# Absorbed queries of a latent-attention kernel, split into high and low parts straight from PSUM by ScalarE and VectorE

## The chip, the cores and the metric

The kernel runs on one core of a Trainium2 chip. The metric is the time of one execution on the device in microseconds (us), as the median of three runs. The engines are named as in the profile: PE is TensorE (PEld its weight loads), DVE is VectorE, ACT is ScalarE, POOL is GpSimd, SP is SyncE.

## The reference, cut to what matters

Two layers of a diffusion backbone are computed for 1024 latent tokens and 128 prompt tokens. The first layer is multi-head latent attention with 16 heads; the change lies in it. Its scores need, for each head, the product of queries and keys, and the keys are an expansion of a compressed latent of 128 numbers:

```
q = (rms_norm(q_a, q_norm_g) @ w_qb).reshape(..., 16, 128 + 64)       # q_nope, q_rope
k_nope, v = split((c_kv @ w_kvb).reshape(..., 16, 128 + 128))
s = (einsum('bqhd,bkhd->bhqk', q_nope, k_nope)
     + einsum('bqhr,bkr->bhqk', q_rope, k_rope)) * MLA_SCALE
p = softmax_f32(s)
o = einsum('bhqk,bkhd->bqhd', p, v)
```

The kernel doesn't expand the keys. It multiplies the query weight of a head with the key weight of that head and applies the product to the low-rank query (256 numbers for each token). The result, an *absorbed query* of 128 numbers for each token and head, is multiplied with the latent itself.

## The kernel before

**Precision.** A float32 operand is split into a high part, rounded to the type fp32r, and a low part, the rest; a product is then three fp32r matmuls (`mm3`: high-high, high-low, low-high). `split_to(hi, lo, src, eng_lo)` (L148) does the split: ACT copies `src` to `hi` with the cast, and then the engine `eng_lo`, POOL unless another is named, subtracts `hi` from `src` and writes `lo` (the helper `sub`, L83).

**The units.** Latent attention runs from about 345 us to 1135 us as a loop over 64 units, unit k = 4 * head + u with u the quarter of 256 latent tokens. Each unit takes about 12.3 us (790 us by 64). While unit k is exponentiated and multiplied with the values, the scores of unit k + 1 are made, their running maximum is taken (`run_max`, L760 to L764 on DVE), the maximum is transposed by PE (`max_cols`, L769), reduced by DVE (L774), turned into a row by PE (L788) and subtracted from the scores by further matmuls (L800). The exponentials are split: cast by ACT (L812), subtraction by DVE (`lo`, L817). POOL adds them up (`sums`, L825 to L830). PE multiplies the last key blocks with the values as whole float32 numbers (L838, called v68 in the orders) and the others in split form (L88 ps_M, called v03 and v45).

**The order is written out.** In this loop every engine runs its instructions in the order in which the program issues them. The order is a string for each k % 8 (`ORDERS`), whose marks are steps: `s` scores, `m` the maximum, `e` the exponential, `h` and `l` the high and low part of the exponentials, `+` the sums, `v` the values, `M` and `L` the way of the maximum and of the row sums (`M0`, `L0` transposes, `M1`, `L1` reductions, `L2`, `L3` the split of the inverse), `F` and `O` the end of the unit before. The parts of the strings of k % 8 = 5 and 6 that matter here:

```
5: ... s2 P m2 T h1 +2 +3 s3 l1 h2 m3 P +4 p s4 m4 l2 v68 ES p  L0 M0 L1 M1 L2 v03 p A L3 ES ...
6: ... s2 p m2 T e4 h1 +2 +3 s3 l1 h2 m3 p +4 s4 m4 l2 v68 ES P M0 P L0 L1 M1 L2 v03 L3 ES A ...
```

**The side work.** The queries of the next heads are made in the gaps of that order, as a queue of items of the type `Work`: `prod` (matmuls into a PSUM bank), `evac` (what takes the result out) and `rest` (what is done with it later). `P` or `p` issues the `prod` of the next item, unless one still waits to be evacuated; `ES` or `EV` issues its `evac` with ACT or DVE as the engine `eng`; `A` issues one step of `rest`. For a head there is one `w_item` (the weight product), three `q_item`s (384 tokens of absorbed queries each: 6 matmuls of 384 columns), and for an even head three `rope_item`s (the rotary queries of two heads); items of the prompt's attention come between.

**One bank.** All these products go to PSUM banks with the tag `W`, and in this stage there is one of them (`psum_plan(M=2, W=1)`; with three of `S`, two of `T` and two of `M` all eight banks are taken). The next `prod` on PE waits until everything that reads the bank's last contents is done.

**The absorbed query before.** `evac` copies the bank to the SBUF tile `qt` (L566 through `copy_by`, L521). `parts`, which an `A` issues later, splits `qt` into the tiles `qA` (two heads' buffers in turn): ACT casts (L149), POOL subtracts (L83). For head 0 alone DVE subtracts (`G_ = V if h == 0 else G`); head 0 is made ahead of the loop, in the region from about 322 to 340 us, where the order is not written out. Items of head 1 to 15, 45 in all, lie in the loop.

Of the kernel before, what the change touches and what calls it, by code (L numbers as in the profile page):

```python
# [11 lines left out]
F32 = mybir.dt.float32  # L12
# [7 lines left out]
P = 128  # L20
# [37 lines left out]
def hybrid_step(ctx: ExitStack, tc: tile.TileContext, i, o):  # L58
    nc = tc.nc
    V, S, G = nc.vector, nc.scalar, nc.gpsimd  # L60
# [15 lines left out]
    def bank(tag):  # L76
        return (psum if tag in "ST" else ps_now["pool"]).tile([P, 512], F32, tag=tag, name=f"ps_{tag}",
                                                               bufs=n_banks[tag])
# [3 lines left out]
    def sub(eng, out, a, b):  # L82
        eng.tensor_tensor(out, a, b, ALU.subtract)  # L83

    def mm3(ps, lhs, rhs, first=True, last=True):

        for n, (a, b) in enumerate(PASSES):
            nc.tensor.matmul(ps, lhs[a], rhs[b], start=first and n == 0, stop=last and n == 2)  # L88
# [59 lines left out]
    def split_to(hi, lo, src, eng_lo=G):  # L148
        S.copy(hi, src)  # L149
        sub(eng_lo, lo, src, hi.bitcast(F32))  # L150
# [369 lines left out]
    def copy_by(eng, out, src):  # L520
        (eng.copy if eng is S else eng.tensor_copy)(out, src)  # L521

    def head_work(h):

        w = {}
        G_ = V if h == 0 else G

        def pair_tiles(a, b, dt=F32):
            if h == 0:
                t = pg.tile([P, 1024], dt, tag="raw", name="w_raw", bufs=4)  # L530
                return t[:, 0:384], t[:, 384:768]
            return [p2.tile([P, 384], dt, tag=x, name=x, bufs=1) for x in (a, b) if x]
        wa = []
        hps[h] = hp = {}

        def w_item():
            c = {}

            def prod():
                wq, wk, w["r"] = head_w.pop(h)  # L540
                c["ps"] = bank("W")[:, :2 * LAT]
                for k in range(2):
                    mm3(c["ps"][:, k * P:(k + 1) * P], [wq[e][:, k * P:(k + 1) * P] for e in range(2)], wk)

            def evac(eng):
                c["t"] = p2a.tile([P, 384], F32, tag="qt", name="qt", bufs=2)[:, :2 * LAT]
                copy_by(eng, c["t"], c["ps"])
            def parts():
                wa.extend(p2a.tile([P, 2 * LAT], F32R, tag=f"wa{e}", name=f"wa{e}", bufs=1) for e in range(2))
                split_to(wa[0], wa[1], c["t"], G_)  # L550
                fresh.add(("wa", h))
            return Work(prod, evac, [parts])

        def q_item(g):
            c = {}
            sl = slice(g * 384, (g + 1) * 384)

            def prod():
                c["ps"] = bank("W")[:, :384]
                for k in range(2):  # L560
                    mm3(c["ps"], [wa[e][:, k * P:(k + 1) * P] for e in range(2)], [qaT[e][:, k, sl] for e in range(2)],
                        k == 0, k == 1)

            def evac(eng):
                c["t"] = p2a.tile([P, 384], F32, tag="qt", name="qt", bufs=2)
                copy_by(eng, c["t"], c["ps"])  # L566
            def parts():
                if g == 0:
                    hp["qA"] = qA_[h % 2]
                    if h % 2 == 1:  # L570
                        hp["q2"] = q2_[h % 3]
                split_to(hp["qA"][0][:, sl], hp["qA"][1][:, sl], c["t"], G_)
                there.add((h, g))
            return Work(prod, evac, [parts], ("wa", h))

        def rope_item(g):
            c = {}
            sl = slice(g * 384, (g + 1) * 384)
            n = 384 if g < 2 else 256
            ls = slice(g * 384, g * 384 + n)  # L580

            def prod():
                wr = w["r"]
                c["ps"] = bank("W")[:, :384]
                for k in range(2):
                    mm3(c["ps"], [wr[e][:, k * P:(k + 1) * P] for e in range(2)], [qaT[e][:, k, sl] for e in range(2)],
                        k == 0, k == 1)
                c["rC"], c["rS"] = pair_tiles("rC", "rS")
                dma(c["rC"][:, :n], i["ropeC"][:, ls])
                dma(c["rS"][:, :n], i["ropeS"][:, ls])  # L590

            def evac(eng):
                c["a"] = p2a.tile([P, 384], F32, tag="qt", name="qt", bufs=2)
                copy_by(eng, c["a"], c["ps"])

            def rotate():
                a, b = c["a"], pair_tiles("rp0", None)[0]
                V.stream_shuffle(b[:, :n], a[:, :n], [x ^ 16 for x in range(32)])
                G_.tensor_tensor(b[:, :n], b[:, :n], c["rS"][:, :n], ALU.mult)
                V.tensor_tensor(a[:, :n], a[:, :n], c["rC"][:, :n], ALU.mult)  # L600
                G_.tensor_tensor(a[:, :n], a[:, :n], b[:, :n], ALU.add)

            def parts():
                a = c["a"]
                t = pair_tiles("rp0", "rp1", F32R)
                split_to(t[0], t[1], a, V)
                if g == 0:

                    hp["q2"] = q2_[h % 3]
                q2 = q2_[h % 3], q2_[(h + 1) % 3]  # L610
                for e in range(2):
                    r = slice(e * 64, e * 64 + 64)
                    dma(q2[e][0][0:64, sl].bitcast(F32), t[0][r].bitcast(F32))
                    dma(q2[e][0][64:128, sl].bitcast(F32), t[0][r].bitcast(F32))
                    dma(q2[e][1][0:64, sl].bitcast(F32), t[1][r].bitcast(F32))
            return Work(prod, evac, [rotate, parts])
        return [w_item()] + [x(g) for g in range(3) for x in ([rope_item] if h % 2 == 0 else []) + [q_item]]
# [270 lines left out]
    p2a = es_a.enter_context(tc.tile_pool(name="p2a", bufs=1, side="right", reuse_waits="tile"))  # L888
# [122 lines left out]
    for k, (h, u) in enumerate(units):  # L1011
# [26 lines left out]
        for step in ORDERS[k % 8].split():  # L1038
# [5 lines left out]
            c, n = step[0], int(step[1:] or 0) if step[1:].isdigit() else step[1:]  # L1044
# [111 lines left out]
    for t in range(NT):  # L1156
        ps = bank("S")[:, :256] if t else early["ps"]
# [234 lines left out]
    for hf in range(2):  # L1392
        for t in range(NT):
            ps = bank("S")
# [391 lines left out]
    for k in range(-2, N):  # L1786
# [22 lines left out]
        for step in NORDER.split():  # L1809
            c, n = step[0], step[1:]  # L1810
# [159 lines left out]
```

## Time and profile before

| | |
|---|---|
| median of 3 runs | 2126.91 us (2126.76 to 2130.87) |
| the profiled execution | 2128.24 us |
| its span in the profile | 2126.5 us |
| PE busy | 2021.3 us, 95% of the span |
| DVE busy | 1358.8 us, 64% |
| ACT busy | 1045.9 us, 49% |
| POOL busy | 824.4 us, 39% |

The span runs from the first to the last instruction that the profile shows; 1.74 us of the profiled execution lie around it. A busy share is a mean over stages with different limits, and the change lies in one stage.

### The profile page before, as it was taken

Reading aid. Unit: us, or ns where it says so; the run is one execution under the profiler, and the core shown is the slowest. Engines: PE = TensorE matmul, PEld = TensorE weight load, DVE = VectorE, ACT = ScalarE, POOL = GpSimd, SP = SyncE. Lnnn points to the kernel's source line nnn. Section 1 sums busy time; section 2 is a strip of 40 time slices with the busy share of each in tenths; the row PEclk is TensorE's granted clock in tenths of the full one; section 3 lists DMA queues with packets and bytes.
Section 4 is the critical chain, followed back from the end, with each engine's and each line's share of the span. In section 5 each row is a group of like instructions: output and inputs, shape, how many; then the busy total and the mean of one; then the engine's idle time right before and its main releaser. Section 6 shows DMA issues by size and latency. Waiting matters only on the chain. (4 is left out here: it accounts for less than half of the span.)

```text
span 2126.5 us, 36852 instructions
## 1 busy us (share of the span) xinstructions
PE 2021.3 (95%) x12894; PEld 1856.7 (87%) x12894; DVE 1358.8 (64%) x2904; ACT 1045.9 (49%) x2430; POOL 824.4 (39%) x822
## 2 busy tenths in 40 slices
PE   8899998999999999999998899999999999999897
PEld 3799998888999998899997788899889999998686
DVE  5723885767787868686776645532116788888743
ACT  6555115554555555555554433433115666666621
POOL 1411224676676768776764300100002333333300
PEclk9999998999999999999999999999999999999899
DMA  8222763212121213121214624326324555556753
GB/s 300 91 74 94 239 174 85 60 50 69 50 76 45 80 32 96 55 80 32 76 31 149 220 103 136 103 100 202 122 104 147 181 178 178 175 176 199 212 156 90
DMA packets 177229, 256.43 MB, mean 121 GB/s; under 512 B 20946, under 2 KB 142578, under 8 KB 177044
## 3 DMA queue, kind: packets, MB, share of 16 engines
q1 hardware_dynamic: 176780, 253.71, 38.4%
q8 instruction: 102, 1.67, 0.3%
q14 instruction: 83, 0.68, 0.1%
q10 hardware_dynamic: 136, 0.26, 0.0%
q0 software_dynamic: 128, 0.11, 0.0%
HBM read 182.58 MB, written 51.49 MB: 110 GB/s over the span
## 5 line engine op out<-in xcount | busy, mean ns | idle before, releaser
L828 POOL TENSOR_TENSOR sm<-sm,pf 128x512 f32<-128x512 f32 (+1 forms) x192 | 260.1, 1354 | 15.8 <-ACT pf L807 1.7
L817 DVE TENSOR_TENSOR pT<-pf,pT 128x512 fp32r<-128x512 f32 x192 | 229.6, 1196 | 41.4 <-ACT pT L812 41.3
L88 PE MATMUL ps_W<-h,w 128*128 128x384 f32 x1152 | 240.2, 348 | 0.4 <-DVE w L83 0.4
L747 PE MATMUL ps_S<-qA,cKT 128*128 128x256 f32 x1152 | 201.2, 294 | 6.3 <-ACT pf L807 6.2
L88 PEld LDWEIGHTS ps_W<-h,w 128*128 128x128 f32 x1152 | 200.5, 191 | 6.4 <-DVE w L83 0.8
L88 PE MATMUL ps_S<-hT,w_hi 128*128 128x384 f32 x720 | 190.1, 342 | 4.3 <-DVE hT L83 2.6
L747 PEld LDWEIGHTS ps_S<-qA,cKT 128*128 128x128 f32 x1152 | 170.2, 191 | 13.4 <-ACT pf L807 10.3
L1656 POOL TENSOR_SCALAR pf<-pf,li 128x512 f32<-128x512 f32 x128 | 90.7, 708 | 204.4 <-DVE li L1653 186.4
L88 PE MATMUL ps_M<-pT,cK 128*128 128x256 f32 x1152 | 164.2, 289 | 0.0
L88 PEld LDWEIGHTS ps_M<-pT,cK 128*128 128x128 f32 x1152 | 146.0, 189 | 0.0
L88 PEld LDWEIGHTS ps_S<-hT,w_hi 128*128 128x128 f32 x720 | 131.3, 189 | 6.4 <-DVE hT L83 3.3
L825 POOL TENSOR_TENSOR sm<-pf 128x512 f32<-128x512 f32 x64 | 86.2, 1347 | 109.7 <-ACT pf L807 109.4
L88 PE MATMUL ps_S<-wo,og 128*128 128x512 f32 x432 | 124.9, 397 | 0.0
L88 PE MATMUL ps_S<-hT,w_lo 128*128 128x384 f32 x360 | 122.4, 341 | 0.0
L521 ACT COPY qt<-ps_W 128x384 f32<-128x384 f32 (+1 forms) x104 | 46.4, 446 | 149.9 <-PE ps_W L88 142.4
L812 ACT CAST pT<-pf 128x512 fp32r<-128x512 f32 x192 | 116.7, 616 | 0.0
L1650 ACT ACTIVATE pf<-pf,nm 128x512 f32<-128x512 f32 x128 | 93.0, 726 | 34.0 <-DVE nm L1647 30.4
L747 PE MATMUL ps_S<-q,KR 128*128 128x256 f32 x384 | 108.5, 283 | 0.0
L807 ACT ACTIVATE pf<-ps_S 128x512 f32<-128x512 f32 x192 | 105.4, 581 | 0.0
L747 PE MATMUL ps_T<-qA,cKT 128*128 128x256 f32 x576 | 102.3, 293 | 0.0
L83 DVE TENSOR_TENSOR og<-w_raw,og 128x512 fp32r<-128x512 f32 x56 | 54.6, 991 | 69.0 <-ACT og L149 68.8
L838 PE MATMUL ps_M<-pf,cKf 128*128 128x256 f32 x384 | 93.4, 379 | 0.0
(378 smaller groups left out, 5047.1 us busy)
## 6 DMA issues: line engine op xcount, KB each, us to landing
w_raw<-in_w_ada SPq DMA_DIRECT2D x48, 512.0 KB
w_raw<-og_d SPq DMA_DIRECT2D x41, 512.0 KB
vw<-vd SPq DMA_DIRECT2D x128, 128.0 KB
bias<-in_bias SPq DMA_DIRECT2D x64, 192.0 KB
q<-rp SPq DMA_DIRECT2D x126, 96.0 KB
gate_d<-gt SPq DMA_DIRECT2D x48, 192.0 KB
w_raw<-in_wgate SPq DMA_DIRECT2D x16, 512.0 KB
gt<-gate_d SPq DMA_DIRECT2D x64, 128.0 KB
```

The source lines that it names most:

```text
L83: eng.tensor_tensor(out, a, b, ALU.subtract)
L88: nc.tensor.matmul(ps, lhs[a], rhs[b], start=first and n == 0, stop=last and n == 2)
L521: (eng.copy if eng is S else eng.tensor_copy)(out, src)
L747: nc.tensor.matmul(ps[:, c:c + 256], k_[:, j, :], q_[:, un["qs"]], start=c == 0 and n == 0, stop=n == 3, skip_group_check=True)
L807: S.activation(pf, un["banks"][b][:, :w], AF.Exp)
L812: S.copy(un["pT"][b][0][:, :pf.shape[1]], pf)
L817: V.tensor_tensor(x[1], pf, x[0].bitcast(F32), ALU.subtract)
L825: G.tensor_tensor(un["sm"], un["pf"][0], pf, ALU.add)
L828: G.tensor_tensor(sm[:, :w], sm[:, :w], pf, ALU.add)
L838: nc.tensor.matmul(un["pso"], cKf[:, j - WHOLE, :], un["pf"][j // 2][:, c], start=j == WHOLE, stop=False)
L1650: S.activation(it["pf", rg], it["pf", rg], AF.Exp, bias=it["nm", rg], scale=1.0, accum_out=it["li", rg])
L1656: G.tensor_scalar(it["pf", rg], it["pf", rg], it["li", rg][:, 0:1], 1.0, ALU.mult, ALU.mult)
```

## The change

The absorbed query is no longer copied. `evac`, which used `eng`, now makes both parts from the bank itself, whatever `eng` is: ACT casts PSUM to `hi`, then DVE subtracts `hi` from PSUM and writes `lo`. `parts` keeps only the mark that the item is there. The tile `qt` is still used by the other items.

```diff
             def evac(eng):
-                c["t"] = p2a.tile([P, 384], F32, tag="qt", name="qt", bufs=2)
-                copy_by(eng, c["t"], c["ps"])
-            def parts():
                 if g == 0:
                     hp["qA"] = qA_[h % 2]
                     if h % 2 == 1:
                         hp["q2"] = q2_[h % 3]
-                split_to(hp["qA"][0][:, sl], hp["qA"][1][:, sl], c["t"], G_)
+                split_to(hp["qA"][0][:, sl], hp["qA"][1][:, sl], c["ps"], V)
+
+            def parts():
                 there.add((h, g))
             return Work(prod, evac, [parts], ("wa", h))
```

## Rows read from the trace of the kernel before

**Rows 1.** Loop: length, busy us of PE, PEld, DVE, ACT, POOL; clock (1.00 full), DMA.

```profile
345.00:1135.00 790.00, 753.80 (x5663) 712.36 (x5663) 587.08 (x1054) 440.10 (x1028) 548.83 (x470) 1.00 0.22 60
```

**Rows 2.** Instructions by tile (qt, then qA): duration ns min/median/max, first and last start, forms.

```profile
L521 ACT COPY qt<-ps_W x104: 349/478/532, 322.1 to 1127.7; 128x384 f32<-128x384 f32 x72, 128x256 f32<-128x256 f32 x32
...
L83 POOL TENSOR_TENSOR qA<-qt,qA x45: 994/1017/1476, 363.5 to 1095.7; 128x384 fp32r<-128x384 f32 x45
...
L83 DVE TENSOR_TENSOR qA<-qt,qA x3: 548/550/553, 328.1 to 340.0; 128x384 fp32r<-128x384 f32 x3
```

**Rows 3.** Waits in the loop: us in total, times, longest us.

```profile
PE ps_M L769 <- DVE rm L764: 14.6, 26, 0.9
PE ps_M L851 <- POOL sm L828: 10.7, 20, 1.4
...
DVE gr L872 <- PE ps_M L866: 90.1, 51, 2.5
```

**Rows 4.** Timeline of unit 29 (k % 8 = 5): start us, us, engine, line, what [idle before].

```profile
713.34 0.48 ACT L521 COPY qt<-ps_W 128x384 f32<-128x384 f32 x1 [0.33 <-PE ps_W L88]
...
714.58 1.46 PE L838 MATMUL ps_M<-pf,cKf 128*128 128x256 f32 x6
...
715.69 1.40 PE L88 MATMUL ps_W<-qaT,wr 128*128 128x384 f32 x6
716.29 1.01 POOL L83 TENSOR_TENSOR qA<-qt,qA 128x384 fp32r<-128x384 f32 x1
716.37 1.22 DVE L762 TENSOR_TENSOR rm<-rm 128x256 f32<-128x256 f32 x1
...
718.03 0.68 DVE L817 TENSOR_TENSOR pT<-pf,pT 128x512 fp32r<-128x512 f32 x1
...
718.17 0.44 PE L769 MATMUL ps_M<-ident,rm 128*128 128x128 f32 x2 [0.86 <-DVE rm L764]
...
718.36 1.68 PE L88 MATMUL ps_M<-pT,cK 128*128 128x256 f32 x12
```

**Rows 5.** Timeline of unit 30 (k % 8 = 6).

```profile
727.90 1.46 PE L838 MATMUL ps_M<-pf,cKf 128*128 128x256 f32 x6
...
729.01 1.40 PE L88 MATMUL ps_W<-qaT,wr 128*128 128x384 f32 x6
...
729.88 0.42 DVE L762 TENSOR_TENSOR rm<-rm 128x256 f32<-128x256 f32 x1
...
730.41 0.42 DVE L764 TENSOR_TENSOR rm<-ps_T,rm 128x256 f32<-128x256 f32 x1
...
730.75 0.69 DVE L817 TENSOR_TENSOR pT<-pf,pT 128x512 fp32r<-128x512 f32 x1
...
730.89 0.44 PE L769 MATMUL ps_M<-ident,rm 128*128 128x128 f32 x2 [0.48 <-DVE rm L764]
...
731.30 1.68 PE L88 MATMUL ps_M<-pT,cK 128*128 128x256 f32 x12
```

**Rows 6.** Second layer, one line's instructions: a subtraction with one operand in PSUM.

```profile
L1450 DVE TENSOR_TENSOR nq<-ps_W,nq x64: 283/488/560, 1587.7 to 1960.3; 64x384 fp32r<-64x384 f32 x32, 64x256 fp32r<-64x256 f32 x16, 64x128 fp32r<-64x128 f32 x16
```

**Rows 7.** Timeline of unit 26 (k % 8 = 2).

```profile
681.14 0.44 PE L769 MATMUL ps_M<-ident,rm 128*128 128x128 f32 x2 [0.45 <-DVE rm L764]
```

**Rows 8.** Timeline of PE outside the loop: three first matmuls after an idle gap.

```profile
66.83 0.44 PE L88 MATMUL ps_S<-hT,w_hi 128*128 128x384 f32 x1 [2.61 <-DVE hT L83]
...
1920.48 0.48 PE L1634 MATMUL ps_S<-nk,nq 128*128 128x512 f32 x1 [2.13 <-DMA nk<-nk]
...
1992.39 0.66 PE L1661 MATMUL ps_T<-ident,pf 128*128 128x128 f32 x4 [1.77 <-POOL pf L1656]
```

**Rows 9.** Busy time and granted clock of the stretches behind those gaps, columns as rows 1.

```profile
66.83:70.30 3.47, 3.47 (x15) 3.13 (x16) 2.55 (x5) 1.19 (x2) 2.27 (x2) 0.71 0.61 250
...
1920.48:1926.00 5.52, 5.52 (x25) 5.29 (x26) 3.17 (x11) 2.05 (x5) 1.82 (x3) 0.69 0.56 191
...
1990.00:1996.00 6.00, 4.23 (x24) 3.11 (x23) 5.77 (x19) 4.55 (x12) 3.00 (x5) 1.00 0.48 157
```

## The prediction

> **What bounds the kernel now.** I read the page first, then the loop of latent attention by windows, since the change touches nothing else but head 0. In the loop PE is busy 753.8 of 790 us at its full clock, and no other engine comes near [rows 1]: PE sets the pace, and the reader should see that 48 fewer copies on ACT and 45 fewer subtractions on POOL are worth nothing by themselves. What counts is the 36 us in which PE stands still, and what would be added to them. The chain of waits gives the two largest items: 14.6 us for the running maximum on DVE, in 26 units, and 10.7 us for the sums on POOL, in 20 [rows 3]. DVE itself stands still at the start of most units until PE has finished the unit before (90.1 us, 51 times) [rows 3]. So DVE's lag begins anew in each unit, and grows inside it until PE waits for the maximum.
>
> Then I followed the queue of side items by hand through the orders, unit by unit, and held the result against the timeline: all copies are on ACT (104 of them) [rows 2], so each of the 45 items of the loop is evacuated at an `ES`. Where this `ES` lies decides what the change does, since DVE now works there too.
>
> **What is removed and added, by duration.** Removed for each of the 45 items are a copy on ACT (0.48 us) and a subtraction on POOL (1.02 us, 45.8 us in all) [rows 2]. The cast moves forward to the place of the copy, at about the copy's price. Added is a subtraction on DVE with one operand in PSUM. The trace has it at 0.56 us for 384 columns on 64 partitions [rows 6], and from SBUF on all 128 at 0.55 [rows 2]: I take 0.55, with 0.49 and 0.56 as bounds. That is 25 us on an engine busy 587 of 790. It hides where DVE has time to spare, and not otherwise.
>
> **What is held longer.** More important is the one bank `W`. Until now it was free when ACT's copy was done; after the change it is free when DVE's subtraction is done, and DVE comes to it only in its own order. The 45 items fall into four groups by what stands ahead of the subtraction on DVE and behind it on PE.
>
> *Six items in units with k % 8 = 5 (13 to 53).* ACT copies at 713.34, when DVE is still far behind. PE has a rotary product of the queue at 715.69, right behind v68, and starts it without waiting [rows 4]. DVE has three steps ahead of the new subtraction: m3, m4 and l2, which ends at 718.03 + 0.68 = 718.71. One thing comes back. The second maximum of m3 takes 1.22 us beside POOL's subtraction on `qA` [rows 4], where it takes 0.42 alone in the next unit [rows 5]; with that subtraction gone l2 ends 0.80 earlier, at 717.91. Add 0.03 to the next instruction, 0.55 for the subtraction and 0.06 to PE (as from the maximum's end at 730.83 to the transpose at 730.89 [rows 5]): PE starts the product at 718.55. Six matmuls of 384 columns at 2.4 GHz are 0.96, the transposes 0.41 (from 730.89 to 731.30 [rows 5]), 0.05 lies between; v03 starts at 719.97 where it was 718.36, and the wait of 0.86 for the maximum is contained in it. The price is 1.6 us, six times: 9.6. Without what comes back it is 2.4.
>
> *Six items in units with k % 8 = 6 (14 to 54).* The same, with the product at 729.01 and l2 ending at 731.44; here POOL's subtraction doesn't lie beside the maximum, and nothing comes back. PE starts at 731.44 + 0.64 = 732.08, v03 at 733.50 instead of 731.30 [rows 5]: 2.2 us, six times: 13.2.
>
> PE issues in order. Behind the waiting product stand both transposes, v03, the last scores, and through them ACT's exponentials; all of these start later, and as DVE starts each unit behind PE, nothing is regained.
>
> *Nine items where the subtraction comes into the chain of the maximum* (k % 8 = 2, and the first items of heads 1 and 3). No product follows at once, but m3, l2 and m4 come 0.55 later, and in unit 26 PE waits 0.45 for m4 already [rows 7]. Between 0.2, if l2 then lies clear of POOL, and 0.55: I take 0.45, together 4.0.
>
> *Nine items ahead of L1 and M1* (k % 8 = 1 and one of head 3). The reduced maximum comes up to 0.55 later, but between the transposes and the point at which PE wants it lies v03, 12 matmuls and over 1.4 us [rows 4, 5], which cover most of that. I take 0.1 each, 0.9 in all; bounds 0 and 0.55.
>
> *Fifteen items behind L3* (k % 8 = 3 and 7, head 2): DVE would stand still there until the unit's end [rows 3], and the next product of the queue is half a unit away. Nothing; without that cover 0.55 each, 8.
>
> Head 0 lies in a region ordered by the tools and bound by the same bank: each handover grows by 0.55, and a copy and its buffer go. Three items, so between -2 and +2; I take 0. POOL's 10.7 us of PE's waiting [rows 3] lie mostly where the exponential comes late, not POOL's subtraction: I take -1, with 0 and -10.7 as bounds.
>
> **POOL and DVE beside each other.** The maximum of 1.22 us in rows 4 is the case to be weighed. The Trainium skill (SBUF — State Buffer, Who interferes with whom) says that a DVE instruction with two SBUF inputs contends with a POOL instruction that reads SBUF, and that one with at most one SBUF input does not. By that rule the new subtraction can't be slowed by POOL, and all that DVE loses beside POOL's 45 subtractions comes back; this is the first rival below. By the rows alone the gain is the 0.80 us, and it is in the sum.
>
> **The clock.** PE would now stand still from about 716.0 to 718.55 in the first group and from 729.36 to 732.08 in the second: 2.5 to 2.7 us, longer than any gap the loop has. Outside the loop a gap of 2.61 us and one of 2.13 [rows 8] are followed by a granted clock of 0.71 and 0.69; behind one of 1.77 it stays at 1.00 [rows 9]. The mean 0.69 over 5.52 us is 3.4 us at the lower level (1.2 of 2.4 GHz): 0.31 * 2 * 5.52. In that time PE does 1.7 us less work. I take such a drop for 8 of the 12 gaps: 13.6; bounds 0 and 20.4. [...]
>
> **The sum.** 9.6 + 13.2 + 4.0 + 0.9 - 1 + 13.6 = 40.3 us on the profiled execution's 2128.24 us: 2168.5. The median of the runs is 1.33 lower, so I predict 2167.
>
> **The rivals.**
> *Faster.* The place is the rotary product behind v68 in the units of the first two groups. If DVE were through with l2 and the subtraction before PE gets there, the bank would cost nothing, and the waits for the maximum and for POOL would shrink: at best 6 * 0.86 and 10.7 less, 2128.2 - 15.9 = 2112, or 2111 as a median. It decides from the point at which l2 ends 3.0 us earlier in unit 29. Against it: only 0.80 us of what is ahead is POOL's doing. Chance 0.03. All of it cancelling out within 0.2%, about what a measurement of this kernel can tell from no change: 0.04.
> *The waits without the clock.* The gaps are 2.5 to 2.7 us, and what the rows show at 2.13 need not hold beside a loop as dense as this one. Then 26.7 us are left: 2155, as a median 2154. Chance 0.22.
> *Every gap drops the clock.* 26.7 + 20.4: 2175, as a median 2174. Chance 0.22. If a second wait then keeps the clock down for twice as long, 20.4 more: 2194. Chance 0.05.
> *Some of the gaps*, the forecast: 0.44.
>
> **Range and chances.** From 2143, no drop of the clock, both small groups at their lower bounds and POOL giving 5 us back (2128.2 + 22.8 + 1.8 - 5 - 1.3 is 2146.5, and 3 for the sizes), to 2184: all 12 drops and both small groups at 0.55 (22.8 + 9.9 + 20.4 + 2 for head 0, less 1.3, is 2182). Slower by over 0.2%: 0.93; within: 0.04; faster: 0.03.
>
> **What would show it.** In the changed profile PE's rotary product (six times in each of the two groups) starts only behind a DVE subtraction on `qA`, at a wait of 2 us or more; POOL has no subtraction on `qA` left; DVE's takes 0.55 from PSUM; the clock of the loop falls from 1.00 to about 0.97. In units 25, 27 and 31 almost nothing moves. I am wrong if DVE reaches the subtraction ahead of l2, if PE's product doesn't wait for it, or if the loop's clock stays at 1.00 and only the 27 us come.

## The result, and the profile after

The change makes the kernel slower by 1.7%: 2163.85 us (median of 4 runs, 2162.38 to 2165.33) against 2126.84 for the kernel before, measured beside it (4 runs, 2123.55 to 2130.87), a ratio of 1.0173 with an interval of 1.0154 to 1.0192. Forecast were 2167 us and a range of 2143 to 2184. The profiled execution of the changed kernel took 2165.33 us (span 2163.5), 37.1 more than that of before.

Part 1 of the page, busy time by engine:

```profile
PE 2038.0 (94%) x12894; PEld 1873.4 (87%) x12894; DVE 1367.5 (63%) x2949; ACT 1024.5 (47%) x2382; POOL 769.8 (36%) x777
```

ACT is 21 us less busy and POOL 55, as the change intends; the time is longer all the same. PE is busy 17 us longer than before with no matmul added, the first sign of a lower clock.

Busy time by window over the loop (columns as in [rows 1]), and the instructions by tile (as [rows 2]):

```profile
345.00:1135.00 790.00, 736.55 (x5432) 697.33 (x5431) 567.88 (x1048) 401.77 (x940) 479.33 (x410) 0.98 0.21 57
```

```profile
L149 ACT CAST qA<-ps_W x48: 454/480/528, 327.6 to 1130.8; 128x384 fp32r<-128x384 f32 x48
...
L83 DVE TENSOR_TENSOR qA<-ps_W,qA x48: 542/551/559, 328.1 to 1132.7; 128x384 fp32r<-128x384 f32 x48
```

In the same 790 us PE now gets through 5432 matmuls instead of 5663, at a clock of 0.98 instead of 1.00. (Before the change this stretch ends with unit 62; the last unit ends at 1147.7 us, so that a unit takes 12.6 us on average.) The cast from PSUM costs what the copy cost, and the subtraction 0.551 us, the 0.55 of the forecast. It stays between 0.542 and 0.559 in all 48 places, 18 of which lie beside work of POOL, while POOL's subtraction went up to 1.476 [rows 2].

The waits of PE in latent attention (as [rows 3]):

```profile
PE ps_W L88 <- DVE qA L83: 29.9, 13, 2.6
PE ps_M L768 <- DVE rm L763: 10.1, 15, 0.8
PE ps_M L850 <- POOL sm L827: 7.1, 17, 1.1
```

A wait that before does not show heads the list: PE wants the bank `W` and DVE's subtraction has not read it yet. Twelve of the 13 last 2.29 to 2.60 us, and they lie in the six units of k % 8 = 5 and the six of k % 8 = 6 that the prediction names (the 13th, 0.69 us, is in unit 8). The waits for the maximum and the sums shrank by 4.5 and 3.6 us.

Units 29 and 30 in the timeline (as [rows 4, 5]):

```profile
728.22 0.48 ACT L149 CAST qA<-ps_W 128x384 fp32r<-128x384 f32 x1 [0.32 <-PE ps_W L88]
...
729.46 1.46 PE L837 MATMUL ps_M<-pf,cKf 128*128 128x256 f32 x6
...
731.25 0.42 DVE L761 TENSOR_TENSOR rm<-rm 128x256 f32<-128x256 f32 x1
...
732.11 0.68 DVE L816 TENSOR_TENSOR pT<-pf,pT 128x512 fp32r<-128x512 f32 x1
...
732.71 0.55 DVE L83 TENSOR_TENSOR qA<-ps_W,qA 128x384 fp32r<-128x384 f32 x1
...
733.32 2.12 PE L88 MATMUL ps_W<-qaT,wr 128*128 128x384 f32 x6 [2.40 <-DVE qA L83]
...
735.94 2.13 PE L88 MATMUL ps_M<-pT,cK 128*128 128x256 f32 x12
...
748.48 0.69 DVE L816 TENSOR_TENSOR pT<-pf,pT 128x512 fp32r<-128x512 f32 x1
...
749.09 0.55 DVE L83 TENSOR_TENSOR qA<-ps_W,qA 128x384 fp32r<-128x384 f32 x1
...
749.69 1.55 PE L88 MATMUL ps_W<-qaT,wr 128*128 128x384 f32 x6 [2.29 <-DVE qA L83]
...
751.74 2.68 PE L88 MATMUL ps_M<-pT,cK 128*128 128x256 f32 x12
```

Read unit 29 down. ACT has read the bank at 728.70. DVE first finishes the maximum and l2 (732.11 + 0.68), subtracts at 732.71, and PE starts at 733.32. Its own work had ended 2.40 earlier. Behind the wait the same six matmuls take 2.12 instead of 1.40, and the next twelve 2.13 instead of 1.68.

The windows of 10 us behind such a wait, in units 29 and 21:

```profile
731.32:741.32 10.00, 8.00 (x51) 7.79 (x52) 5.00 (x14) 3.06 (x8) 2.95 (x3) 0.83 0.11 34
626.39:636.39 10.00, 8.00 (x64) 7.84 (x65) 6.05 (x16) 4.60 (x11) 4.16 (x4) 1.00 0.20 57
```

Eight of the twelve windows show 0.83 or 0.84, four show 1.00. A mean of 0.83 over 10 us is 3.4 us at 1.2 of 2.4 GHz (0.17 * 2 * 10).

Where the time was lost can be taken unit by unit: the start of the matmul that ends each unit (L866 before, L865 after), after minus before, and the growth of that difference from unit to unit. For unit 29 these are, before and then after:

```profile
708.67 0.28 PE L866 MATMUL ps_M<-row,onesR 128*128 128x256 f32 x1
...
722.00 0.28 PE L866 MATMUL ps_M<-row,onesR 128*128 128x256 f32 x1
```

```profile
723.55 0.28 PE L865 MATMUL ps_M<-row,onesR 128*128 128x256 f32 x1
...
740.03 0.28 PE L865 MATMUL ps_M<-row,onesR 128*128 128x256 f32 x1
```

The change is 14.88 us late where unit 28 ends and 18.03 where unit 29 does, so unit 29 loses 3.15. The twelve units hold 33.65 of the 37.1 us. The first unit already ends 3.07 late (at 358.90 where it was 355.83). What is left nearly cancels. In units 37 and 38 PE also waits for POOL's sums before the change (0.59 and 0.75 us), and the two divide their loss otherwise than the other five pairs; prices per unit below are those of the five pairs, sums take all twelve.

### The profile page after: what moved, and what is told of

The parts are those of the page before. It is cut to its first block, busy times and chain, and to the rows that moved or that the text cites. A ratio compares the mean times of both kernels' runs of the same rounds, so it can differ in the third digit from the quotient of the medians.

```text
span 2163.5 us, 36775 instructions
## 1 busy us (share of the span) xinstructions
PE 2038.0 (94%) x12894; PEld 1873.4 (87%) x12894; DVE 1367.5 (63%) x2949; ACT 1024.5 (47%) x2382; POOL 769.8 (36%) x777
## 3 DMA queue, kind: packets, MB, share of 16 engines
q8 instruction: 102, 1.67, 0.3%
## 4 chain that ended last, share of the span: by engine, by line
PE 43%; DVE 4%; DMA 3%; ACT 3%; POOL 2%; issue 2%; SPq 0%; DVEq 0%; ACTq 0%; POOLq 0%
PE ps_S L88 16%; PE ps_W L88 11%; PE ps_M L88 5%; PE ps_M L1685 2%; PE ps_T L1660 2%; POOL sm L827 1%; PE ps_S L746 1%; PE ps_S L1633 1%; PE ps_S L1634 1%; DMA w_raw<-in_wout 1%; DVE og L83 1%; DVE rm L759 1%; ACT pf L806 1%; DMA vw<-vd 1%; PE ps_S L799 1%
## 5 line engine op out<-in xcount | busy, mean ns | idle before, releaser
L816 DVE TENSOR_TENSOR pT<-pf,pT 128x512 fp32r<-128x512 f32 x192 | 223.3, 1164 | 43.1 <-ACT pT L811 43.1
L88 PE MATMUL ps_M<-pT,cK 128*128 128x256 f32 x1152 | 171.5, 297 | 0.0
L88 PEld LDWEIGHTS ps_M<-pT,cK 128*128 128x128 f32 x1152 | 153.4, 198 | 0.0
L759 DVE TENSOR_TENSOR rm<-ps_S,rm 128x512 f32<-128x512 f32 x128 | 87.5, 683 | 9.0 <-PE ps_S L746 4.2
```

Source lines behind the costliest of these rows:

```text
L759: V.tensor_tensor(rm, ps, rm, ALU.max)
L816: V.tensor_tensor(x[1], pf, x[0].bitcast(F32), ALU.subtract)
```

## The experiments

Two questions were open. The first is what makes PE late. *The bank*: DVE's place in the order frees the bank late. *DVE's work*: 25 us more on DVE, in the chain of the maximum, make the time. The second is the clock: either its drops behind the waits cost some 12 us of the 37, or the waits alone cost it all.

**The subtraction ahead of the maximum.** A new mark `Q` in the orders of k % 8 = 5 and 6 issues the evacuation of an absorbed query between h2 and m3; the next product stays where it was.

```diff
-5: ... s3 l1 h2 m3 P +4 p s4 m4 l2 v68 ES p L0 M0 ...
-6: ... s3 l1 h2 m3 p +4 s4 m4 l2 v68 ES P M0 P L0 ...
+5: ... s3 l1 h2 Q m3 P +4 p s4 m4 l2 v68 ES p L0 M0 ...
+6: ... s3 l1 h2 Q m3 p +4 s4 m4 l2 v68 ES P M0 P L0 ...
...
+    def do_early():
+
+        if pend and pend[0].needs and pend[0].needs[0] == "wa":
+            pend[0].evac(S)
+            early_out["q"] = 1
...
+            elif c == "Q":
+                do_early()
```

> The changed kernel with one thing moved: in the orders of k % 8 = 5 and 6 the cast and the subtraction of the absorbed query are issued before m3, not behind l2 and v68; PE's order is untouched. If the cost is the bank held until DVE is through with m3, m4 and l2 (theory), the 12 waits of 2.3 to 2.6 us at the rotary product vanish or shrink under 0.5 us and the clock of the loop is back at 1.00: 2128 to 2136 us. If the cost is DVE's added work of 25 us (rival), the time stays at 2160 to 2166.

Measured: 2131.45 us (10 runs) against 2128.68 for before (19 runs), a ratio of 1.0013 (1.0002 to 1.0024). The wait and the product in unit 30, from the timeline:

```profile
730.73 1.75 DVE L825 TENSOR_TENSOR pT<-pf,pT 128x512 fp32r<-128x512 f32 x1
732.40 0.55 DVE L83 TENSOR_TENSOR qA<-ps_W,qA 128x384 fp32r<-128x384 f32 x1
...
733.00 1.32 PE L88 MATMUL ps_W<-qaT,wr 128*128 128x384 f32 x6 [0.37 <-DVE qA L83]
```

And the waits of PE:

```profile
PE ps_W L88 <- DVE qA L83: 4.9, 13, 0.9
```

Eleven of the twelve waits are 0.18 to 0.43 us long, and the one of unit 38 is 0.90; none is followed by a drop of the clock. The same instructions on the same engines, with nothing but the place of the cast in ACT's order and of the subtraction in DVE's changed, are 0.02 to 0.24% slower than before: 32 of the 37 us are gone. It is the place of the subtraction, not its being there.

**The copy kept, DVE subtracts.** The kernel before, with POOL's subtraction moved to DVE; the bank is free behind ACT's copy.

```diff
-                split_to(hp["qA"][0][:, sl], hp["qA"][1][:, sl], c["t"], G_)
+                split_to(hp["qA"][0][:, sl], hp["qA"][1][:, sl], c["t"], V)
```

> The kernel before with one thing changed: the low part of the absorbed query is subtracted by DVE from the SBUF copy, not by POOL; the copy stays and frees the bank. DVE has the added work of the change, the bank isn't held. Theory (the bank): 2123 to 2132 us. Rival (DVE's added work sets the time): 2150 or more.

Measured: 2131.73 us (10 runs), a ratio of 1.0018 (1.0005 to 1.0031). The loop by windows:

```profile
345.00:1135.00 790.00, 755.43 (x5635) 712.29 (x5635) 596.83 (x1091) 442.35 (x1029) 504.20 (x428) 0.99 0.22 60
```

DVE, now with all 45 subtractions, is 10 us busier in the window than before [rows 1], and the time is 0.05 to 0.31% longer. Unit by unit, k % 8 = 5 gains 0.8 us each (the maximum free of POOL), k % 8 = 6 loses 0.17, k % 8 = 1 mostly 0.5 and k % 8 = 2 mostly 0.25. The theory that DVE's added work as such makes the time falls. Here, though, DVE subtracts later than in the change; the next experiment keeps the change's place.

**A bank held, with nothing else changed.** The kernel before, with a subtraction of one column on DVE that reads the bank behind ACT's copy (45 items; its result isn't used).

```diff
                 copy_by(eng, c["t"], c["ps"])
+                if h:
+                    x = p2a.tile([P, 1], F32, tag="touch", name="touch", bufs=2)
+                    V.tensor_tensor(x, c["ps"][:, 0:1], c["t"][:, 0:1], ALU.subtract)
```

> The kernel before with one small DVE instruction added: at the place where the absorbed query is evacuated DVE reads one column of the bank (heads 1 to 15), so that the bank is held until DVE comes there, and DVE has hardly more work. Copy, cast and POOL's subtraction stay. Theory (the bank): the 12 waits at the rotary product are there, some 2 us each, with drops of the clock behind most: 2150 to 2165 us. Rival (DVE's added work): 2126 to 2131.

Measured: 2172.37 us (4 runs), a ratio of 1.0194 (1.0172 to 1.0216): right in direction and more than I had expected. The waits and the loop:

```profile
PE ps_W L88 <- DVE touch L569: 28.8, 13, 2.8
```

```profile
345.00:1135.00 790.00, 730.03 (x5366) 690.00 (x5365) 565.02 (x1037) 420.71 (x978) 522.72 (x452) 0.97 0.21 57
```

The same 13 waits, about as long in all as with the change, though DVE's added work is one column, 0.15 us each time. Nothing comes back here, as POOL keeps its subtractions: units of k % 8 = 5 lose 2.0 us without a drop of the clock (units 13 and 45 4.7 and 3.5 with the clock down). Of k % 8 = 6, unit 14 loses 1.5 without a drop and the other five 2.3 to 3.3 with one. The twelve lose 32.6 together. Five units of k % 8 = 2 lose 0.9 each, and unit 2, with a drop, 2.4, which I hadn't counted. So the holding of the bank, with hardly any work added, makes a loss of this size.

**The clock held up.** The changed kernel with 18 matmuls of 256 columns ahead of each of the twelve waiting products, into the unused half of an accumulation bank. PE then has work in the gap, and the product starts no earlier.

```diff
+FILL = 18
...
+                q = pend and pend[0].needs and pend[0].needs[0] == "wa"
                 do_evac({"V": V, "S": S}[n])
+                if q and k > 12 and k % 8 in (5, 6):
+                    for _ in range(FILL):
+                        nc.tensor.matmul(un["pb"][:, 256:512], cK[0][:, 0, :], un["pT"][0][0][:, 0:256],
+                                         start=False, stop=False, skip_group_check=True)
```

> The changed kernel with 18 more matmuls of 256 columns, into a part of a PSUM bank that nobody reads, in each of the 12 places where PE waits for the bank, ahead of the waiting product: 1.9 us of work into gaps of about 2.7 us. If the lower clock behind 8 of the gaps costs some 1.6 us each (theory), the clock stays at 1.00 and the time falls by 10 to 16 us, to 2148 to 2154. If the gaps alone are the cost and the clock costs nothing (rival), it stays at 2162 to 2166.

Measured: 2152.22 us (4 runs, 2150.52 to 2155.1), a ratio of 1.0108 (1.0088 to 1.0127). Unit 30 in the timeline, the window behind its product, and the waits of PE:

```profile
727.86 2.51 PE L1057 MATMUL ps_M<-pT,cK 128*128 128x256 f32 x18
730.61 1.32 PE L89 MATMUL ps_W<-qaT,wr 128*128 128x384 f32 x6 [0.24 <-DVE qA L84]
...
732.12 1.67 PE L89 MATMUL ps_M<-pT,cK 128*128 128x256 f32 x12
```

```profile
730.61:740.61 10.00, 10.00 (x78) 9.84 (x79) 6.32 (x13) 6.61 (x16) 6.09 (x5) 1.00 0.30 89
```

```profile
PE ps_W L89 <- DVE qA L84: 4.8, 13, 0.7
```

The product still starts behind DVE's subtraction, so the bank costs what it did; but the twelve matmuls behind it take 1.67 us as before the change, and all twelve windows of 10 us behind these products show a clock of 1.00. Units of k % 8 = 5 lose 1.58 to 1.60 us and of k % 8 = 6 2.14 to 2.19 (37 and 38: 2.07 and 1.42). Work without any use makes the changed kernel 11.6 us faster (2163.85 - 2152.22): the clock's share. The two medians were not measured beside each other; by the ratios to before, 1.0173 and 1.0108, it is some 14 us, and unit by unit in the profiles 11.4.

**Half of that filling.** The same with 9 matmuls, which leaves part of the gap.

```diff
-FILL = 18
+FILL = 9
```

> As the filled kernel, with 9 matmuls of 256 columns instead of 18 in each of the 12 gaps: about 1.0 us of work, so that PE stands still for some 1.5 us where it was 2.4. Outside the loop gaps of up to 1.8 us left the clock at 1.00. Theory: no drops in the loop, 2150 to 2155 us. Rival (what counts is the whole of the wait, or the place): drops at several of the 12, 2156 to 2165.

Measured: 2151.37 us (4 runs) against 2126.3 (15 runs), a ratio of 1.0124 (1.011 to 1.0138). The waits of PE, and the windows behind the gap of unit 30 and behind another one, of 1.14 us in unit 10:

```profile
PE ps_W L89 <- DVE qA L84: 17.7, 13, 1.5
```

```profile
747.45:757.45 10.00, 10.00 (x81) 9.85 (x82) 6.45 (x14) 6.24 (x15) 5.65 (x5) 1.00 0.32 85
485.80:495.80 10.00, 9.55 (x66) 9.08 (x67) 5.09 (x12) 5.08 (x12) 2.94 (x3) 0.83 0.09 26
```

The twelve gaps are now 1.28 to 1.52 us long, and again all twelve windows behind them show 1.00: the units of the two groups lose 1.55 to 1.61 and 2.16 to 2.20 us (37 and 38: 2.07 and 1.37). The medians of the two fillings agree within 1 us. The theory had no drops in the whole loop, and that is wrong: this profile has three elsewhere, in units 7, 10 and 62, behind gaps of 1.13, 1.14 and 1.60 us; unit 10 lost 1.5 by it.

**The product later.** The changed kernel, with the product that waits taken from behind v68: to the other marks of the unit in k % 8 = 5, behind v03 in k % 8 = 6.

```diff
-5: ... v68 ES p L0 M0 L1 M1 L2 v03 p A L3 ES ...
-6: ... v68 ES P M0 P L0 L1 M1 L2 v03 L3 ES ...
+5: ... v68 ES L0 M0 L1 M1 L2 v03 p A L3 ES ...
+6: ... v68 ES M0 L0 L1 M1 L2 v03 P L3 ES ...
```

> The changed kernel with PE's side product of the orders k % 8 = 5 and 6 issued behind v03 and not behind v68, DVE's order as changed. Theory: PE no longer waits for the bank, but it now waits for the maximum at the transposes, which the product used to cover: about 0.5 us more than in the kernel before at k % 8 = 5 and 1.0 at 6, without drops of the clock: 2133 to 2142 us. Rival (the subtraction ahead of L1 and M1 costs as much wherever the product is): 2150 or more.

Measured: 2150.12 us (4 runs), a ratio of 1.0116 (1.0098 to 1.0134): some 8 us above what I had expected at most, and in the range of the rival. Unit 30 in the timeline, the window behind its wait, and the waits of PE:

```profile
741.70 0.57 PE L768 MATMUL ps_M<-ident,rm 128*128 128x128 f32 x2 [1.95 <-DVE rm L763]
...
742.17 0.55 DVE L83 TENSOR_TENSOR qA<-ps_W,qA 128x384 fp32r<-128x384 f32 x1
...
742.35 2.91 PE L88 MATMUL ps_M<-pT,cK 128*128 128x256 f32 x12
...
745.06 1.33 PE L88 MATMUL ps_W<-qaT,wr 128*128 128x384 f32 x6
```

```profile
741.70:751.70 10.00, 9.93 (x66) 9.58 (x67) 5.72 (x14) 4.88 (x12) 4.01 (x4) 0.83 0.22 66
```

```profile
PE ps_M L768 <- DVE rm L763: 25.3, 29, 2.0
...
PE ps_W L88 <- DVE qA L83: 0.7, 1, 0.7
```

The wait for the bank is gone, as meant, and the units of k % 8 = 5 lose 0.47 us (unit 37 1.58, with a wait of 1.59 for the sums). In k % 8 = 6 the product had covered DVE's lag: without its 1.40 us the transposes wait 1.95 for the maximum, where they waited 0.48 [rows 5]. Most of the 1.47 more is the time that the product used to fill, and the product itself now comes on top, behind v03. These units lose 1.69 without a drop of the clock and 3.2 with one (unit 38 3.5), and four of the six drop (window 0.83). Taking the bank's wait away by moving PE's work turned it into another wait at the same place. The rival's reason isn't borne out: at L1 and M1 the subtraction still stands where it did, and in units 22 and 54, with 1.7 lost each, PE's only wait is the one for the maximum ahead of it. The forecast failed by the length of that wait and by the drops.

**Head 0 as before.** The changed kernel, in which only the items of head 1 to 15 come straight from the bank.

```diff
+    def straight(h, g):
+        return h > 0
+
+    def copy_dve(h, g):
+        return False
...
-                split_to(hp["qA"][0][:, sl], hp["qA"][1][:, sl], c["ps"], V)
+                c["to"] = hp["qA"][0][:, sl], hp["qA"][1][:, sl]
+                if straight(h, g):
+                    split_to(*c["to"], c["ps"], V)
+                    return
+                c["t"] = p2a.tile([P, 384], F32, tag="qt", name="qt", bufs=2)
+                copy_by(eng, c["t"], c["ps"])
...
             def parts():
+                if not straight(h, g):
+                    split_to(*c["to"], c["t"], V if copy_dve(h, g) else G_)
```

> The changed kernel with head 0 left as before (copy, then cast and DVE's subtraction from SBUF); heads 1 to 15 as changed. If head 0 costs some 2 us in the region ahead of the loop (from its last transpose to the first of the last scores 22 us against 19 to 20), that comes back: 2160 to 2163 us, and that region is 19 to 20 us long. If the difference there is mere scatter of the starts (rival), the region stays at 21 to 22 us.

Measured: 2163.68 us (4 runs, 2158.79 to 2168.0), the median of the change itself and a little above the range expected. The transposes of the first maximum, which wait for head 0's last item, in the change and here:

```profile
342.39 0.44 PE L768 MATMUL ps_W<-ident,rm 128*128 128x128 f32 x2 [1.16 <-DVE qA L83]
```

```profile
340.78 0.44 PE L781 MATMUL ps_W<-ident,rm 128*128 128x128 f32 x2 [0.57 <-ACT qt L521]
```

From the last transpose ahead of head 0's products (L234, or the same line moved by one) to the first matmul that subtracts the maximum, the region is 18.97 to 20.53 us long in the five profiles in which head 0 is copied (before and four of the variants; mean 19.65), and 20.97 to 22.28 in the five in which it is not (mean 21.55). The clock plays into it: in four of the ten (the change among them) the mean granted clock from 322 to 336 us is 0.63, in the six others (before among them) 0.76. Among those at 0.76 the region is 19.0 to 19.3 us against 21.0 to 21.2, among those at 0.63 it is 20.5 against 22.3. So head 0 costs 1.8 to 2.0 us in the profiles, as expected of the region; in the total this is within the runs' scatter.

**By place.** For the heads above 3 the three items of a head are told apart: those of k % 8 = 5 keep their copy and DVE subtracts later (the gain that the second experiment showed), the third items of these heads and all of head 2 come straight from the bank, the rest is as before.

```diff
+    def straight(h, g):
+        return h == 2 or h > 3 and g == 2
+    def copy_dve(h, g):
+        return h > 3 and h % 2 == 0 and g == 0
...
+                if straight(h, g):
+                    split_to(*c["to"], c["ps"], V)
+                    return
...
+                if not straight(h, g):
+                    split_to(*c["to"], c["t"], V if copy_dve(h, g) else G_)
```

> A mixture by place: the items of k % 8 = 5 keep the copy and let DVE subtract from it later; head 2 and the third item of every later head (behind L3) are made straight from PSUM; all others stay as in the kernel before. Theory (each place has its own price, as the units of the earlier runs show: about -0.8 us at k % 8 = 5, nothing behind L3, -1.5 at head 2): 2120 to 2126 us beside 2127 to 2129 for the kernel before, faster by 0.1 to 0.35%. Rival (the gains belong to the whole arrangement and not to the place): within 0.1%.

Measured: 2125.57 us (11 runs, 2120.41 to 2125.78) against 2126.3 (15 runs), a ratio of 0.9993 (0.9984 to 1.0002). That is inconclusive: no change at all lies within the interval. In its one profile the units of k % 8 = 5 gain 0.8 us each (unit 37 0.2) and units 7 and 43 0.6 each; from the end of the first unit, 3.57 us late, to that of the last, 1.17 early, it gains 4.7 us. Whether this version beats before can't be said from these runs.

## Why the prediction was right, step by step

*The waits, 9.6 + 13.2.* Right. PE waited in the twelve units named, for the instruction named. Where the clock doesn't drop, k % 8 = 5 lost 1.58 us each (forecast 1.6) and k % 8 = 6 2.17 (2.2), read from the filled kernels in five of the six pairs; the twelve sum to 22.27 there, against 22.8. The holding of the bank was shown to be the cause from both sides: the bank held with one column of work makes the same 13 waits, and the subtraction moved ahead of m3 takes 32 of the 37 us away.

*The 0.80 that comes back from POOL.* Right in five of the six units: with POOL's subtraction gone the second maximum of unit 29 takes 0.42 us, where it took 1.22 [rows 4]. In unit 37 it took 0.42 before the change too, so that nothing came back there, and it lost 2.07. Where POOL kept its subtraction (the bank touched by one column) these units lost 2.0 instead of 1.58. The Trainium skill (SBUF — State Buffer, Who interferes with whom) lets a DVE instruction with one SBUF input run beside POOL unhindered; the trace agrees, with 0.542 to 0.559 us for the 18 new subtractions that lie beside POOL's work and 0.543 to 0.558 for the other 30.

*The clock, 13.6.* The mechanism is right, and the size was a little too large. That eight of the twelve gaps would drop the clock was taken without a working of its own; that it came out at exactly eight is luck. The loss in the twelve units is 33.65 - 22.27 = 11.4 us, 1.4 for each drop instead of 1.7, and the filled kernel gives 11.6 by the medians. Filling the gap with useless work removes it, so it is the clock and no second wait. Why four gaps of the same length left none is open. The Trainium skill (TensorE: Matmul & The Clock Gate, HAM oscillation) has a kernel pay for the lower clock behind each of its waits, which last some 3 to 5 us there. The waits here, of 2.3 to 2.6 us, are shorter, and eight of the twelve were paid for all the same.

*The chain of the maximum, 4.0.* Mis-sized: about 2, with 0.3 and 0.8 in units 1 and 8, 0.5 in unit 58 and 0.1 or less in the others. The step took 0.45 for each on the ground that PE waits for m4 already in unit 26. The wait for the maximum there did grow, from 0.45 to 0.76; but PE comes to it 0.2 sooner, as the transposes of the sums ahead of it start sooner, and the maximum itself is only 0.1 later. The 0.8 of unit 8 is of another kind: the step said that no product follows at once, and there one did. It is the 13th wait for the bank, 0.69 us.

*Ahead of L1 and M1, 0.9.* The cover was whole: about 0. *Behind L3, 0.* Right.

*Head 0, 0.* About +1.9 in the profiles, just inside the ±2 of the forecast. At the last handover of the bank PE's wait grew from 0.57 to 1.16 us, as the step had it; no gain from the copy and the buffer that go is seen beside it.

*POOL, -1.* About -2: 0.85, 0.62 and 0.64 in units 6, 7 and 43.

In sum, 40.3 us were forecast on the profiled execution and 37.1 came: the clock and the chain of the maximum were sized too high by some 2 us each, and head 0 set off a part. Two things that the sum didn't have came with this profile: about 1 us lost to a lower mean clock ahead of the loop (0.63 against 0.76), and 0.8 in unit 62, behind a gap that before has as well. That the total came so close is thus in part errors that cancel.

Of the rivals, *the waits without the clock* (2154) is what the filled kernels are, at 2151 to 2152, and the change isn't. *Every gap drops the clock* falls by the four windows at 1.00. *Faster* would have needed DVE to pass l2 before PE reaches the product; the 3.0 us given for it left out the subtraction itself, with which it is 3.7 (718.71 + 0.64 - 715.69). Put in front by hand, ahead of m3, it takes the wait away but gives no gain: units of k % 8 = 5 are then 0.35 us shorter than before the change, units of k % 8 = 6 0.6 longer.

## What to carry to other kernels

A buffer of which there is one is free when its last reader has run, and the reader's place in its own engine's order counts for more than its duration: ask what stands ahead of it there, and what stands behind the next writer. A copy that looks superfluous can be what frees the bank early, here worth 1.6 to 2.2 us for each of the twelve items with a product close behind, and more where the wait costs the clock; for the other items it was worth little or nothing. Before work is moved away from a wait, look whether it covered a second one.

## What the runs showed of the hardware that was not expected

Gaps of nearly one length on PE went both ways. Of the twelve gaps of 2.3 to 2.6 us in the loop, eight were followed by 3.4 us at the lower of the two clock levels and four by none. In the profile of the variant that copies head 0 alone it was eight of the same twelve again, with unit 21 in the place of unit 13. In the variant with the product moved, the gaps at the transposes in k % 8 = 6 were 1.57 to 1.96 us long, and the clock fell behind four of the six, the one of 1.57 among them. Of the twelve gaps of 1.28 to 1.52 us in the half-filled kernel none dropped it, while two of 1.13 and 1.14 us in the same profile were followed by a drop, and the gap of 1.77 in [rows 8] had left it at 1.00 [rows 9]. The plainest case is a gap in unit 62 that every version has, for the same exponential, here before and after the change:

```profile
1124.11 0.62 PE L747 MATMUL ps_S<-qA,cKT 128*128 128x256 f32 x3 [1.62 <-ACT pf L807]
```

```profile
1160.36 1.01 PE L746 MATMUL ps_S<-qA,cKT 128*128 128x256 f32 x3 [1.62 <-ACT pf L806]
```

Behind the first the clock stays at 1.00, behind the second it is 0.84 over 10 us; of the ten profiles five are of either kind. So the length of a gap alone didn't decide it here. And 18 useless matmuls of 256 columns, 2.51 us of PE in each gap, made the kernel 11.6 us faster, by the medians, than leaving PE idle.
